# Ordering the output projection's block loads behind the kept weight parts in the SyncE queue, and moving the eight items they belong to

## The chip, the cores and the metric

The kernel runs on one core of a Trainium2 chip. The metric is the device time of one execution in microseconds (us); lower is better. Every engine of the core (TensorE = PE, VectorE = DVE, ScalarE = ACT, GpSimd = POOL, SyncE = SP) works through its own instruction stream in order and waits for the others by semaphores. Here SP issues most loads, and POOL issues most stores to device memory.

## The reference

Two decoder layers are computed on one sequence of 2048 tokens with 1024 channels. The first layer uses a gated matrix memory (mLSTM), the second a linear recurrence. What matters here is the first layer's input projection and, much later, its output projection:

```python
def mlstm_mixer(u, w_in, conv_w, conv_b, w_q, w_k, w_v, b_i, b_f, norm_w, skip, w_out):
    proj = u @ w_in
    xm, z, o_pre, i_pre, f_pre = jnp.split(proj, [...], axis=-1)
    xc = jax.nn.silu(causal_dwconv(xm, conv_w, conv_b))
    ...
    y = (hn + skip * xc) * jax.nn.silu(z)
    return y @ w_out          # (2048 x 2048) @ (2048 x 1024)
```

## The kernel before

**Numbers.** All products are float32 products made of three passes: each operand is split into a high part (a cast on ACT, L759) and a low part (a subtraction on DVE, L762), and `mm3` (L359 to L361) issues high·high, high·low and low·high.

**Products.** Each 2x2 block product uses seven block products in place of eight. This needs four sums of weight blocks, s1 to s4. Where weights serve twice, the split sums are written to device memory once and read back ("kept") later: `kept` (L96) loads 512 KB into one of eight `s` slots (L98).

**Stages.** `phase_a1` computes the input projection in two slabs of 1024 tokens. Slab 0 splits the weights and writes the sums; slab 1 reads the kept sums. In each slab, six z groups come first in two passes (an "early" pass for the first two products, then six "late" groups of five products, 60 matmuls of 512 columns each). Then the list `middle` follows, 14 items: q0, s0, q1, s2, q2, s4, q3, s6, s8, s10, s12, s14, s13, s15. A q item is a group of the o projection with 336 matmuls of 258 columns; an s item is a group of xm (even number: with a convolution on DVE) or z, with 84 matmuls of 512 columns. After `phase_a1` come the recurrence (`phase_a2`) and the second layer.

**The loads that are changed.** Slab 1 also prepares the kept sums of `w_out` for the output projection of a later stage. There are eight rounds, one per block row k. A round has two halves. `wout_blocks` (L463) loads four blocks of 256 KB into four of the eight `x` buffers (L468, on SP). `wout_sums` (L471) forms four sums on DVE (L474, in the order 21+22, 11-21, 22-11, 12-...), splits them (L759 on ACT, L762 on DVE, with four more `x` buffers), and stores eight pieces of 256 KB (L482 and L483, on POOL) to `d_ws`. The list `spread` (L623) says at which items of `middle` a round's loads are called; its sums are called at the next item, just after the weights of that item have been taken.

**What sets the order.** The order on each engine is not that of the Python calls. The tile framework's scheduler puts an instruction where it expects its inputs and its buffer to be ready. Nothing tied L468 to anything, so the scheduler was free to move it ahead of its item. The method `order(first, then)` of the kernel (L765) adds a dependency without a semaphore between two instructions of one engine: it only fixes which stands first in that engine's stream.

**Slots.** A kept load waits on SP until a matmul product has released its `s` slot, and L468 waits until its `x` buffer is free. Both stand in the one SP stream, so what is behind them waits too. On DVE the adds that empty the PSUM banks (L271 for z and s items; L560, L566 and L543 for q items) share the stream with L474.

Of the kernel before, what the change touches and what calls it, by code (L numbers as in the profile page):

```python
# [7 lines left out]
F32 = mybir.dt.float32  # L8
# [30 lines left out]
class Slab:  # L39
# [55 lines left out]

    def kept(self, keep, w=512):  # L96
        both = self.slot(w)
        self.nc.sync.dma_start(both.bitcast(F32), keep)  # L98
        return both[:, 0:w], both[:, w:2 * w]

    def weights(self, src, keep, again, part=None):
# [205 lines left out]
class Trunk:  # L307
# [74 lines left out]
    def phase_a1(self, xT, woq, wxz, wout, D):  # L382
        tc, nc = self.tc, self.nc
        with ExitStack() as ctx:
            S = Slab(self, ctx, "g0")
# [77 lines left out]
            def wout_blocks(k):  # L463

                A = {}
                for nm, kk, c in (("11", k, 0), ("21", k, 512), ("22", k + 8, 512), ("12", k + 8, 0)):
                    A[nm] = S.x()
                    nc.sync.dma_start(A[nm], wout[kk, :, c:c + 512])  # L468
                return A

            def wout_sums(k, A):  # L471
# [146 lines left out]
            for k in range(KD):  # L618
                S.scale(xs, None, pb, (k,))
                nm = ("u11", "u21")[k // 4]  # L620
                U[nm, k % 4] = S.operand(nm, k % 4, xs[k], "v")
            ew = []
            spread, sums = (0, 2, 3, 5, 7, 8, 10, 11), []  # L623
            for s in range(2):
                t = []

# [10 lines left out]
                for j, (kind, i) in enumerate(middle):  # L637
# [3 lines left out]
                    if s == 1 and j in spread:  # L641
                        sums.append((spread.index(j), wout_blocks(spread.index(j))))
# [690 lines left out]
    def phase_b2(self, rgate, rwout, D, outT):  # L1333
# [4 lines left out]
        with ExitStack() as ctx:  # L1338
# [14 lines left out]
            def fetch(kind, b, i):  # L1353

                m = 768 if kind == "g" else 512
                pool = gp if kind == "g" else wp
                keep = D["gw" if kind == "g" else "ow"][i]
                if b > 0:
                    both = pool.tile([P, 2 * m], F32R, tag="w" + kind, name="w" + kind)
                    nc.sync.dma_start(both.bitcast(F32), keep)  # L1360
                    return both[:, 0:m], both[:, m:2 * m]
                raw = pool.tile([P, m], F32, tag="wr" + kind, name="wr", bufs=2)
                nc.gpsimd.dma_start(raw, rgate[i // 2, :, i % 2 * 768:(i % 2 + 1) * 768] if kind == "g" else
                                    rwout[i % NT, :, i // NT * 512:(i // NT + 1) * 512])
                kept(1)
                both = pool.tile([P, 2 * m], F32R, tag="w" + kind, name="w" + kind)
                a = self.split_into(both[:, 0:m], both[:, m:2 * m], raw, "a", "v")
                if kind == "g" and i == 0:
                    self.order(a, self.tail[-4:])
                if kind == "r" and i == 0:  # L1370
                    self.order(self.first, a)
                stores.append((keep, both))
                if i == (7 if kind == "g" else 23):
                    kept(0)
                return both[:, 0:m], both[:, m:2 * m]
# [284 lines left out]
```

## Time and profile before

| | us |
|---|---|
| three timed runs | 3030.61 to 3032.81, median 3031.76 |
| the profiled execution, its own time | 3039.57 |
| its span, first to last instruction | 3037.8 |
| PE busy (95% of the span) | 2874.6 |
| DVE busy | 2130.9 |
| ACT busy | 1517.5 |
| POOL busy | 453.6 |

The mean granted TensorE clock of the profiled execution is 0.975 of full speed. Busy shares are means over stages that are bound by different things, so the stage of the change has to be looked at by itself: slab 1 of `phase_a1`, from about 540 to 1042 us after the span's start. The first of the 32 loads of L468 is issued at 543.8 us and the last at 675.8 us; the 32 sums of L474 run from 553.6 to 686.8 us. This is the stretch of the six late groups of slab 1.

### The profile page before, as it was taken

The page shows a single profiled execution, that of the slowest core. Times are in us where ns is not written, and L with a number is a line of the kernel's source. Part 1 is how long each engine was busy: PE and PEld are TensorE (multiplying, and loading weights), DVE is VectorE, ACT ScalarE, POOL GpSimd, SP SyncE. Part 2 cuts the span into 40 slices and gives each one's busy share as a digit, 9 for nine tenths or more (in the row PEclk, how much of TensorE's full clock was granted, in tenths as well). Part 3 has the DMA queues.
Part 4 walks back from the last instruction along what each step waited for, and adds up shares of the span by engine and source line. Part 5 has one row for each costly group of instructions (what it writes and reads, how often), then busy time and mean ns, then how long its engine had stood idle before and what let it go on. Part 6 is the DMA issues. An engine that isn't in the chain of part 4 may idle for free. (4 is left out here: it accounts for less than half of the span.)

```text
span 3037.8 us, 43242 instructions
## 1 busy us (share of the span) xinstructions
PE 2874.6 (95%) x15442; PEld 2460.0 (81%) x15442; DVE 2130.9 (70%) x3596; ACT 1517.5 (50%) x2557; POOL 453.6 (15%) x870
## 2 busy tenths in 40 slices
PE   7999999879999999999999899999999998799997
PEld 5799987659997799898999777887888886587885
DVE  7766798544447588888888755778889374766763
ACT  6344555323334466666666533435445234777760
POOL 1211132221002111111111201001221111210000
PEclk9999999989999999999999899999999999899998
DMA  6767676887667744545444567686766657778864
GB/s 225 266 217 249 234 253 235 282 315 227 218 215 232 235 147 142 166 131 169 128 146 142 193 218 281 209 272 201 255 230 217 211 185 250 260 273 298 297 203 164
DMA packets 289783, 667.70 MB, mean 220 GB/s; under 512 B 28576, under 2 KB 107168, under 8 KB 289568
## 3 DMA queue, kind: packets, MB, share of 16 engines
q1 hardware_dynamic: 219952, 422.03, 43.8%
q0 software_dynamic: 69040, 241.87, 21.1%
q8 instruction: 121, 1.98, 0.3%
q10 hardware_dynamic: 576, 1.05, 0.1%
q14 instruction: 94, 0.77, 0.1%
HBM read 427.66 MB, written 237.17 MB: 219 GB/s over the span
## 5 line engine op out<-in xcount | busy, mean ns | idle before, releaser
L759 ACT CAST s<-raw 128x512 fp32r<-128x512 f32 (+1 forms) x280 | 172.2, 621 | 267.2 <-PE pc L361 69.1
L762 DVE TENSOR_TENSOR s<-raw,s 128x512 fp32r<-128x512 f32 (+1 forms) x280 | 191.2, 688 | 53.7 <-ACT s L759 52.5
L359 PE MATMUL acc<-yh,wr 128*128 128x512 f32 x384 | 153.9, 408 | 23.3 <-DMA wr<-d_ow 8.9
L360 PE MATMUL acc<-yl,wr 128*128 128x512 f32 x384 | 155.3, 404 | 0.6 <-DVE yl L762 0.6
L361 PE MATMUL acc<-yh,wr 128*128 128x512 f32 x384 | 154.9, 403 | 0.0
L686 DVE SCALAR_TENSOR_TENSOR xc<-xm,vec,xc 128x512 f32<-128x512 f32 x192 | 139.5, 747 | 10.9 <-ACT xc L684 8.4
L759 ACT CAST u<-t 128x512 fp32r<-128x512 f32 x112 | 68.8, 619 | 154.8 <-PE pc L361 51.0
L762 DVE TENSOR_TENSOR u<-t,u 128x512 fp32r<-128x512 f32 x112 | 76.7, 689 | 85.2 <-ACT u L759 84.9
L759 ACT CAST s<-sum 128x512 fp32r<-128x512 f32 (+1 forms) x120 | 74.0, 618 | 116.0 <-PE pc L361 46.4
L359 PE MATMUL pa<-u,s 128*128 128x512 f32 x304 | 122.1, 402 | 4.6 <-ACT p L258 3.1
L360 PE MATMUL pa<-u,s 128*128 128x512 f32 x304 | 121.6, 400 | 0.0
L361 PE MATMUL pa<-u,s 128*128 128x512 f32 x304 | 121.4, 400 | 0.1
L971 DVE SCALAR_TENSOR_TENSOR C<-C,dl,kv 128x516 f32<-128x516 f32 x112 | 83.5, 746 | 48.4 <-PE kv L361 48.4
L759 ACT CAST Ch<-C 128x516 fp32r<-128x516 f32 x120 | 74.8, 623 | 84.5 <-DVE da L989 69.8
L686 DVE SCALAR_TENSOR_TENSOR xc<-xr,vec,xc 128x512 f32<-128x512 f32 x144 | 105.8, 746 | 9.2 <-ACT xc L684 8.3
L359 PEld LDWEIGHTS acc<-yh,wr 128*128 128x128 f32 x384 | 74.4, 195 | 43.3 <-issue 9.3
L359 PE MATMUL pj<-vwh,xmh 128*128 128x512 f32 x256 | 103.1, 403 | 1.9 <-ACT vwh L759 1.9
L360 PE MATMUL pj<-vwl,xmh 128*128 128x512 f32 x256 | 100.5, 393 | 0.8 <-DVE vwl L762 0.8
L361 PE MATMUL pj<-vwh,xml 128*128 128x512 f32 x256 | 100.8, 394 | 0.0
L762 DVE TENSOR_TENSOR s<-sum,s 128x512 fp32r<-128x512 f32 (+1 forms) x120 | 82.5, 688 | 25.2 <-ACT s L759 24.5
L359 PE MATMUL gate<-xch,wg 128*128 128x512 f32 x192 | 78.4, 412 | 16.9 <-ACT xch L759 11.7
L360 PEld LDWEIGHTS acc<-yl,wr 128*128 128x128 f32 x384 | 74.7, 195 | 19.2 <-DVE yl L762 1.5
(483 smaller groups left out, 10097.4 us busy)
## 6 DMA issues: line engine op xcount, KB each, us to landing
wr<-d_ow SPq DMA_DIRECT2D x72, 512.0 KB, 4.3
d_wx<-s POOLq DMA_DIRECT2D x64, 512.0 KB, 4.4
s<-d_wx SPq DMA_DIRECT2D x64, 512.0 KB, 4.7
s<-d_ws SPq DMA_DIRECT2D x64, 512.0 KB, 6.2
raw<-in_wxz_dram SPq DMA_DIRECT2D x124, 256.0 KB, 4.5
d_wr<-s POOLq DMA_DIRECT2D x48, 512.0 KB, 3.7
s<-d_wr SPq DMA_DIRECT2D x48, 512.0 KB, 4.3
raw<-in_rwin_dram SPq DMA_DIRECT2D x94, 256.0 KB, 3.9
```

What stands on the lines that cost most here:

```text
L359: mm(out, sh, mh, start=first, stop=False, skip_group_check=resumed)
L360: mm(out, sh, ml, start=False, stop=False, skip_group_check=resumed)
L361: mm(out, sl, mh, start=False, stop=last, skip_group_check=resumed)
L686: nc.vector.scalar_tensor_tensor(out, x[:, j:j + TB], self.v(wn, m * 4 + j), out, op0=ALU.mult, op1=ALU.add)
L759: a = nc.scalar.copy(hi, src)
L762: b = (nc.gpsimd if lo_eng == "p" else nc.vector).tensor_tensor(lo, src, hi.bitcast(F32), op=ALU.subtract)
L971: nc.vector.scalar_tensor_tensor(C2, C2, self.dl[:, r:r + 1], p2, op0=ALU.mult, op1=ALU.add)
```

## The change

```diff
     def kept(self, keep, w=512):
         both = self.slot(w)
-        self.nc.sync.dma_start(both.bitcast(F32), keep)
+        self.got = self.nc.sync.dma_start(both.bitcast(F32), keep)
         return both[:, 0:w], both[:, w:2 * w]
...
                 for nm, kk, c in (("11", k, 0), ("21", k, 512), ("22", k + 8, 512), ("12", k + 8, 0)):
                     A[nm] = S.x()
-                    nc.sync.dma_start(A[nm], wout[kk, :, c:c + 512])
+                    self.order((S.got,), (nc.sync.dma_start(A[nm], wout[kk, :, c:c + 512]),))
                 return A
...
-            spread, sums = (0, 2, 3, 5, 7, 8, 10, 11), []
+            spread, sums = (0, 1, 2, 4, 5, 6, 8, 10), []
```

`kept` now remembers the load it issued last (`got`). At the moment `wout_blocks` is called at item j, the weights of item j+1 have been requested as well (two items are held ready), so `got` is the last kept part (s4) of item j+1. The four loads of L468 may not stand ahead of it in SP's stream any more. The second edit moves the rounds to other items: loads at q0, s0, q1, q2, s4, q3, s8 and s12, sums at s0, q1, s2, s4, q3, s6, s10 and s14.

The scheduler's result on SP, at the start of the late groups of slab 1 (`s<-d_wx` are kept parts, L98; `raw<-in_woq_dram` are unsplit weights for q0):

```order
 L98 DMA s<-d_wx 128x1024 x3
 L424 DMA raw<-in_woq_dram 128x516
-L98 DMA s<-d_wx 128x1024 x2
-L468 DMA x<-in_wout_dram 128x512 x2
-L98 DMA s<-d_wx 128x1024
-L468 DMA x<-in_wout_dram 128x512
-L98 DMA s<-d_wx 128x1024
-L468 DMA x<-in_wout_dram 128x512
-L424 DMA raw<-in_woq_dram 128x516
```

All 32 loads of L468 stood between the kept parts of the late groups and those of q0. After the change these rows are kept parts and raw weights alone.

DVE in the first of the late groups and at the start of the second (L271 are the adds that read the PSUM banks pb, pc and pd; the split of raw weights is `s<-raw,s`):

```order
 L271 TENSOR_TENSOR u_5638<-pb,p_5276 128x512
-L474 TENSOR_TENSOR x<-x 128x512 x2
 L271 TENSOR_TENSOR p_5276<-pc,u_5638 128x512
-L474 TENSOR_TENSOR x<-x 128x512 x2
-L762 TENSOR_TENSOR x<-x 128x512
 L271 TENSOR_TENSOR z<-pd,p_5276 128x512
-L762 TENSOR_TENSOR x<-x 128x512 x3
 L271 TENSOR_TENSOR z<-pc,u_5638 128x512
 L271 TENSOR_TENSOR z<-pd,u_5638 128x512
-L474 TENSOR_TENSOR x<-x 128x512 x2
```

Sums and splits stood between the adds; now the adds stand alone there. On PE the products of the late groups stay in the same order.

SP at the change from q0 to s0, the first round's new place (`d_o<-os` are stores of the o projection, `s<-d_wq` kept parts of q1; the kept part in the second row is s4 of s0):

```order
 L530 DMA d_o<-os 128x2x256
 L98 DMA s<-d_wx 128x1024
-L530 DMA d_o<-os 128x2x256
-L83 DMA raw<-in_wxz_dram 128x512
-L424 DMA raw<-in_woq_dram 128x516 x3
+L468 DMA x<-in_wout_dram 128x512
+L83 DMA raw<-in_wxz_dram 128x512
+L468 DMA x<-in_wout_dram 128x512 x3
+L424 DMA raw<-in_woq_dram 128x516
+L530 DMA d_o<-os 128x2x256
+L424 DMA raw<-in_woq_dram 128x516 x2
 L98 DMA s<-d_wq 128x1032 x4
```

The four block loads come right behind s4 of s0, ahead of the raw weights and kept parts of q1.

DVE in s0 after the change (before it, these rows held no L474 and no `x<-x`):

```order
+L271 TENSOR_TENSOR u_6748<-pb,p_6733 128x512
+L762 TENSOR_TENSOR s<-raw,s 128x516
+L474 TENSOR_TENSOR x<-x 128x512
+L585 COPY xm<-hist 128x3
+L474 TENSOR_TENSOR x<-x 128x512 x2
+L271 TENSOR_TENSOR p_6733<-pc,u_6748 128x512
+L762 TENSOR_TENSOR s<-raw,s 128x516
+L474 TENSOR_TENSOR x<-x 128x512
+L762 TENSOR_TENSOR x<-x 128x512 x4
+L586 COPY hist<-xm 128x3
+L686 SCALAR_TENSOR_TENSOR xc<-xm,vec,xc 128x512
+L271 TENSOR_TENSOR xm<-pd,p_6733 128x512
```

Three sums now stand between the add of pb and the add of pc, and one sum, four splits and a convolution step between the add of pc and that of pd. The items s2 and s4 have the same pattern; in s6 the sums stand ahead of the add of pb, in s10 they stand among the convolution steps ahead of it, and in s14 they stand around it.

## The prediction

> **What bounds the kernel now.** I read the slices of the span first, because the busy shares alone (PE 95%) hide where PE loses time.
>
> ```profile
> PE   7999999879999999999999899999999998799997
> PEclk9999999989999999999999899999999999899998
> ```
>
> Each digit stands for a fortieth of the span, 75.9 us. PE is full nearly everywhere, so only dips are worth anything. One lies in the eighth and ninth slices (532 to 683 us), where the granted clock drops too. That is where the 32 block loads and their sums run. So I looked at this stretch item by item. Each window below runs from one item's first matmul to the next one's: the six late groups of slab 1, q0, then as measures of a clean item q1, q2 and s6. The columns are the window, its length, the busy time and count of each engine, the granted clock, the DMA share and GB/s.
>
> ```profile
> core 0: us, PE busy (x) PEld busy (x) DVE busy (x) ACT busy (x) POOL busy (x), PEclk, DMA share, GB/s
> 548.80:562.67 13.87, 13.87 (x61) 11.26 (x60) 11.70 (x19) 5.52 (x10) 5.74 (x11) 1.00 0.93 302
> 562.67:585.94 23.27, 16.18 (x62) 12.67 (x60) 8.87 (x14) 4.70 (x8) 6.62 (x13) 0.85 0.90 323
> 585.94:606.37 20.43, 15.74 (x61) 12.32 (x60) 8.08 (x13) 4.06 (x7) 5.33 (x10) 0.92 0.80 270
> 606.37:634.35 27.98, 18.44 (x61) 13.90 (x60) 14.63 (x23) 7.43 (x13) 8.69 (x17) 0.82 0.96 336
> 634.35:657.70 23.35, 15.89 (x61) 12.54 (x60) 10.27 (x16) 5.84 (x10) 7.69 (x15) 0.85 0.82 274
> 657.70:674.75 17.05, 14.19 (x61) 11.20 (x60) 9.53 (x15) 5.42 (x9) 6.12 (x12) 1.00 0.85 305
> 674.75:723.82 49.07, 42.61 (x338) 42.39 (x337) 18.01 (x40) 14.02 (x30) 4.81 (x9) 0.93 0.77 263
> 743.29:783.61 40.32, 40.32 (x337) 40.31 (x336) 18.36 (x41) 13.79 (x29) 2.15 (x4) 1.00 0.71 229
> 803.15:843.32 40.17, 40.17 (x337) 40.17 (x336) 18.35 (x41) 13.80 (x29) 2.15 (x4) 1.00 0.71 229
> 904.24:924.11 19.87, 19.87 (x88) 15.75 (x86) 15.93 (x47) 8.57 (x14) 2.15 (x4) 1.00 0.64 191
> ```
>
> A late group is 60 matmuls. The first takes 13.87 us with PE never idle; the next five take 23.27, 20.43, 27.98, 23.35 and 17.05 us for the same work, 112.08 in place of 69.35. q0 takes 49.07, where q1 and q2 take 40.25 on average. So 42.73 + 8.82 = **51.55 us** are lost here. Behind q0, PE is busy for the whole of each window.
>
> Who is waited for is in the waits, narrowed to 548 to 700 us: first PE's, then DVE's, then SP's (total, times, longest).
>
> ```profile
> PE pc L359 <- DVE p L271: 28.6, 5, 7.5
> PE oa L359 <- ACT p L554: 6.5, 1, 6.5
> PE pd L359 <- DVE z L271: 3.1, 1, 3.1
> ...
> DVE x L474 <- DMA x<-in_wout_dram: 62.2, 7, 12.9
> ...
> SPq L468 <- DMA d_ws<-x: 61.5, 19, 11.6
> ```
>
> PE waits for a DVE add; DVE has been standing at a sum whose block has not landed; the block is late because SP stood at L468 until the last round's stores to d_ws had freed an `x` buffer. One such wait, in order of time on DVE and PE:
>
> ```profile
> 573.61 1.42 DVE L474 TENSOR_TENSOR x<-x 128x512 f32<-128x512 f32 x2 [10.05 <-DMA x<-in_wout_dram]
> 574.95 0.68 DVE L271 TENSOR_TENSOR u<-pb,p 128x512 f32<-128x512 f32 x1
> ...
> 577.48 0.68 DVE L271 TENSOR_TENSOR p<-pc,u 128x512 f32<-128x512 f32 x1
> ...
> 578.30 0.77 PE L359 MATMUL pc<-t4h,s 128*128 128x512 f32 x1 [7.09 <-DVE p L271]
> ```
>
> The add of pb stood behind the sum, the add of pc behind that, and PE may not go on in pc before it is read. The adds to z in pd stand in the same stream, and ACT, whose copy q0 waits for, casts the same sums in order; I take all three rows as one cause. These idle waits make 38.2 us; the rest of the 51.55 is slower matmuls after each wait, which the clock column shows (0.82 to 0.93). After a short wait there is next to none of this: the group at 657.70 holds one wait of 2.86 us, lost 3.18, and its clock stayed at 1.00.
>
> ```profile
> 669.13 0.47 PE L359 MATMUL pc<-t4h,s 128*128 128x512 f32 x1 [2.86 <-DVE p L271]
> ```
>
> **The change, part by part.** Nothing is added or removed in amount: 32 loads, 32 sums, 32 splits and 64 stores, all moved. The handle kept by `kept` costs nothing.
>
> *What goes.* The late groups keep adds and z stores only, and SP has no L468 there. DVE's 8 to 15 us per group fall to about 4, and the first late group shows that 13.87 us is reached even with block loads under way (DMA share 0.93). I take the whole 51.55 us as gained, since nothing else there has ended a PE wait of note. What would be late next is a kept part; those had to wait in the same SP queue until now, and go ahead sooner.
>
> *What comes.* Eight rounds lie in the middle stage, where PE has no idle time: any PE wait costs in full. A round brings this much DVE work:
>
> ```profile
> L474 DVE TENSOR_TENSOR x<-x 128x512 f32<-128x512 f32 x32 | 22.1, 689 | 62.8 <-DMA x<-in_wout_dram 62.2
> L762 DVE TENSOR_TENSOR x<-x 128x512 fp32r<-128x512 f32 x32 | 20.6, 683 | 0.0
> ```
>
> Four of each make 4 x (0.689 + 0.683) = 5.49 us on DVE. The casts on ACT and the store issues on POOL fall to engines that are idle for more than half of each item.
>
> *Rounds in s0, s2, s4.* What such an item does at its second product, without a round, is shown by s2 (SP: s4 of this item, then a raw load; DVE: a split, the add of pd; PE: first matmuls that need the adds of pc and of pd).
>
> ```profile
> 783.09 0.32 SPq L98 DMA_DIRECT2D s<-d_wx  x1
> 785.24 0.42 SPq L83 DMA_DIRECT2D raw<-in_wxz_dram  x1
> ...
> 790.09 0.69 DVE L762 TENSOR_TENSOR s<-raw,s 128x516 fp32r<-128x516 f32 x1
> ...
> 797.93 0.68 DVE L271 TENSOR_TENSOR xm<-pd,p 128x512 f32<-128x512 f32 x1
> ...
> 797.55 0.39 PE L359 MATMUL pc<-t4h,s 128*128 128x512 f32 x1
> 800.35 0.40 PE L359 MATMUL pd<-u22h,s 128*128 128x512 f32 x1
> ```
>
> DVE would reach the first sum at 790.78. Three sums and the add of pc end at 793.5, against 797.55 needed. Then come a split, the fourth sum, four splits (4.1 us) and a convolution step (0.75), so the add of pd ends near 799.1, against 800.35. So 1.2 us are spare. The load that the first sum needs goes out third, near 786.3. How long do loads take? The medians from issue to landing, in the middle stage (first row) and in 540 to 700 us (second and third):
>
> ```profile
> s<-d_wx SPq DMA_DIRECT2D x40, 512.0 KB, 4.2
> ...
> x<-in_wout_dram SPq DMA_DIRECT2D x32, 256.0 KB, 7.9
> d_ws<-x POOLq DMA_DIRECT2D x64, 256.0 KB, 5.6
> ```
>
> With 4.2 us the block lands before DVE asks. With 7.9 it lands at 794.2, 3.4 us late, and PE waits 2.2. So a round costs 0 to 2.2 us; I take 0.7, nearer to the middle stage's own row, since the DMA share there is 0.64 to 0.71 and was 0.80 to 0.96 in the late groups. Three rounds: 2.1, range 0 to 6.6.
>
> *Rounds in q1 and q3.* A q item leaves DVE idle for 22 of its 40 us, and its adds sit in four banks apiece. The same bounds serve, 0 to 2.2; I take 0.5. Two rounds: 1.0, range 0 to 4.4.
>
> *Rounds in s6, s10, s14.* These have s items for neighbours. DVE is busy 15.93 of 19.87 us in s6; with 5.49 more it is 21.42, so 1.55 us too much. At best the next item's slack takes it (0); at worst it adds to a late block (1.55 + 2.2 = 3.75). I take 1.55: 4.65 for three, range 0 to 11.25.
>
> **The sum.** -51.55 + 2.1 + 1.0 + 4.65 = -43.8 us, with bounds -51.55 and -51.55 + 22.25 = -29.3. On the profiled execution's 3039.57 that is 2995.8. This execution lay 7.8 us above the median of the runs, 3031.76; I carry the difference over unchanged, so from the median the forecast is **2988**, with 2980.2 to 3002.5 from the bounds.
>
> **The rivals.**
>
> *B, the loads are slow in the middle stage as well (0.18).* The bytes moved there, with 743 to 904 us of before in the first row and 540 to 700 us in the second:
>
> ```profile
> DMA packets 16073, 35.34 MB, mean 219 GB/s; under 512 B 1618, under 2 KB 7506, under 8 KB 16059
> ...
> DMA packets 17299, 48.31 MB, mean 302 GB/s; under 512 B 2504, under 2 KB 2789, under 8 KB 17291
> ```
>
> A round moves 12 pieces of 256 KB, 3.15 MB. Five rounds in the 161 us make 35.34 + 15.7 = 51.1 MB, 317 GB/s, more than the late groups' mean. So blocks may land as late as there, and all upper bounds hold: -29.3 us, **3002**. Against it: at 229 GB/s the middle stage's DMA share is 0.71, so there is room for some 320 at a full share, and the five rounds are not all in flight at once. The Trainium skill speaks for this rival: "DMA: Bandwidth & Descriptors", section "Issuing engines are not separate DMA queues", says that transfers started by any engine share the same 16 DMA engines and interleave. By it the new place in SP's stream protects nothing from POOL's stores, and the sum would be 3002 where mine is 2988. The trace agrees so far that block loads took 7.9 us where the stores to d_ws ran.
>
> *C, SP stands at L468 again (0.08).* The closest two rounds are those that load in the middle of q1 and at the start of s2 (and likewise q3 and s6). Their places in SP's stream in before, and the first loads of two rounds in the late groups:
>
> ```profile
> 578.79 0.33 SPq L468 DMA_DIRECT2D x<-in_wout_dram  x1
> 598.64 0.33 SPq L468 DMA_DIRECT2D x<-in_wout_dram  x1
> ...
> 760.05 1.04 SPq L98 DMA_DIRECT2D s<-d_wq  x2
> ...
> 783.09 0.32 SPq L98 DMA_DIRECT2D s<-d_wx  x1
> ```
>
> The places are 23 us apart, and a turn of the `x` buffers took 19.85. With the longest group, 27.98, as the turn, two rounds are 5 us later, and the sums with them: 10 us, **2998**.
>
> *D, the late groups stay slow for another reason (0.06).* A kept part could wait for its slot there. I price it at half the gain, 26 us: **3014**, with the rounds' cost. The first late group at 13.87 us speaks against it.
>
> *E, slower than before (0.03).* The DMA engines become the bound of the middle stage. From 723.82 to 904.24 us, 180.4 us at 219 GB/s are 39.5 MB; six rounds add 18.9. At the middle stage's 229 GB/s as a ceiling, 58.4 MB take 255 us, 74.6 more than before, and 23 are left after the gain: **3055**. It decides from 252 GB/s down. The late groups moved 302, so this needs a traffic mix that is much worse.
>
> **How the numbers follow.** My case has 0.62, B 0.18, C 0.08, D 0.06, E 0.03; 0.03 is left for no change to speak of. The range 2978 to 3006 goes 2 us beyond the ceiling of the gain, about the spread of the timed runs, and covers B and C. A difference of 0.2%, 6 us, is about what a measurement of this kernel can tell from none. Faster by more: my case, B, C and D, 0.94; within it 0.03; slower 0.03.
>
> **What would show it.** Six late groups of 13.9 us and a q0 of 40.3, clock 1.00; no wait of DVE for a block before q0; in the middle stage, waits of PE for DVE of 0 to 2 us per round, most in s6, s10 and s14. It is wrong if SP's waits for d_ws go on in tens of us, if block loads take over 8 us, or if an item of the middle stage grows by more than 4 us.

## The result, and the profile after

| | before | after |
|---|---|---|
| median of the timed runs, us | 3032.28 (3030.61 to 3036.26, 4 runs) | 2995.22 (2993.59 to 2996.22, 4 runs) |
| the profiled execution, us | 3039.57 | 2996.22 |
| its span, us | 3037.8 | 2994.5 |

The ratio is 0.9875, with a 95% interval of 0.9858 to 0.9892. The medians differ by 37.1 us, the two profiled executions by 43.35.

The slices of the span of the changed kernel, PE's busy tenths and its granted clock, in fortieths of 74.9 us:

```profile
PE   7999999999999999999999899999999998699997
PEclk9999999999999999999999899999999998799998
```

The dip in the eighth and ninth slices is gone, and the clock stays up. Item by item, in the same columns as before: the first, second and last late group, q0, then q1, s2 and s6, and the whole middle stage from s0 to the start of the recurrence.

```profile
548.92:562.80 13.88, 13.88 (x61) 11.27 (x60) 6.91 (x11) 3.25 (x6) 2.17 (x4) 1.00 0.72 217
562.80:576.72 13.92, 13.92 (x61) 11.27 (x60) 4.11 (x6) 2.52 (x4) 1.63 (x3) 1.00 0.75 237
618.50:632.46 13.96, 13.96 (x62) 11.28 (x60) 4.78 (x7) 3.15 (x5) 1.63 (x3) 1.00 0.69 213
632.46:672.70 40.24, 40.24 (x338) 40.24 (x336) 13.30 (x32) 12.36 (x26) 0.54 (x1) 1.00 0.62 198
692.41:733.47 41.06, 40.57 (x337) 40.36 (x336) 23.39 (x50) 15.96 (x34) 8.22 (x16) 1.00 0.93 327
733.47:753.90 20.43, 19.80 (x86) 15.71 (x85) 13.58 (x29) 9.65 (x16) 5.37 (x10) 1.00 0.82 274
856.44:880.45 24.01, 21.84 (x89) 16.75 (x87) 19.89 (x56) 10.88 (x18) 6.48 (x12) 0.93 0.94 345
672.70:1001.29 328.59, 321.67 (x1861) 280.07 (x1859) 212.15 (x458) 143.17 (x250) 73.40 (x136) 0.99 0.85 288
```

The late groups run at 13.9 us and q0 at 40.24: 548.92 to 672.70 is 123.78 us, where the same work took 175.02 (548.80 to 723.82). That is 51.2 us gained. The middle stage took 319.60 before, in the same window (its row stands with the experiments), so 9.0 are given back. 51.2 - 9.0 = 42.2 us is nearly the whole 43.3 us by which the spans differ; the rest lies behind the start of the recurrence.

The waits of the changed kernel, from the late groups to the recurrence: PE for DVE, and DVE for a block. The second group of rows is the issues, with their size and median time to landing, from 632 to 1001 us.

```profile
PE pd L359 <- DVE xm L271: 2.8, 2, 2.2
...
DVE x L474 <- DMA x<-in_wout_dram: 12.9, 7, 3.4
```

```profile
s<-d_wx SPq DMA_DIRECT2D x40, 512.0 KB, 5.2
d_ws<-x POOLq DMA_DIRECT2D x64, 256.0 KB, 6.7
...
x<-in_wout_dram SPq DMA_DIRECT2D x32, 256.0 KB, 6.0
```

DVE still stands at seven of the eight rounds, but for 12.9 us in place of 62.2. SP no longer stands at L468 for stores to d_ws (61.5 us before): between 632 and 1001 us it waits there twice, 0.8 us together, for stores of xm. Nearly half of the 9 us are lost in s6 (24.01 us against 19.87). On DVE, in order of time:

```profile
862.89 0.69 DVE L474 TENSOR_TENSOR x<-x 128x512 f32<-128x512 f32 x1 [1.61 <-DMA x<-in_wout_dram]
...
869.04 0.67 DVE L271 TENSOR_TENSOR u<-pb,p 128x512 f32<-128x512 f32 x1
...
874.98 0.68 DVE L271 TENSOR_TENSOR xm<-pd,p 128x512 f32<-128x512 f32 x1
```

and on PE:

```profile
875.71 0.50 PE L359 MATMUL pd<-u22h,s 128*128 128x512 f32 x1 [2.17 <-DVE xm L271]
```

The add of pb comes at 869.04, 6.8 us after pb was complete (862.25), because the whole round stands ahead of it. On DVE the small operations of the gates, a split and steps of the convolution follow, so the add of pd is late too. PE waits 2.17 us for it, and the matmuls behind that run at a lower clock.

### The profile page after: what moved, and what is told of

Its sections match the earlier page's. It is cut to its first block, busy times and chain, and to the rows that moved or that the text cites. A ratio compares the mean times of both kernels' runs of the same rounds, so it can differ in the third digit from the quotient of the medians.

```text
span 2994.5 us, 43193 instructions
## 1 busy us (share of the span) xinstructions
PE 2861.5 (96%) x15442; PEld 2448.8 (82%) x15442; DVE 2127.1 (71%) x3596; ACT 1517.2 (51%) x2557; POOL 455.6 (15%) x870
## 5 line engine op out<-in xcount | busy, mean ns | idle before, releaser
L360 PE MATMUL pd<-u,s 128*128 128x512 f32 x224 | 88.5, 395 | 2.0 <-DVE u L762 2.0
```

The costliest lines, as they stand in the source:

```text
L360: mm(out, sh, ml, start=False, stop=False, skip_group_check=resumed)
```

## The experiments

Two stretches are compared throughout. The first is the six late groups with q0; the 123.78 us of the changed kernel are its clean length. The second is the middle stage, with 319.60 us in the kernel before.

| run | late groups and q0, us | over 123.8 | middle stage, us | over 319.6 | time, us |
|---|---|---|---|---|---|
| before | 175.02 | +51.2 | 319.60 | 0 | 3032.28 median |
| after | 123.78 | 0 | 328.59 | +9.0 | 2995.22 median |
| before_again | 171.66 | +47.9 | 319.59 | 0 | 3033.20 |
| spread_only | 171.15 | +47.4 | 319.87 | +0.3 | 3029.14 |
| order_only | 123.77 | 0 | 327.35 | +7.8 | 2990.52 median |
| before_no_sums | 143.42 | +19.6 | 319.85 | +0.3 | 3003.21 |
| before_no_sums_pool | 134.34 | +10.6 | 319.61 | 0 | 3000.89 |
| no_sums | 123.77 | 0 | 319.65 | 0 | 2986.03 |
| no_loads_pinned | 123.77 | 0 | 322.83 | +3.2 | 2988.52 |
| late_three | 125.32 | +1.5 | 320.16 | +0.6 | 2988.38 median |

**before_again**, the kernel before with no edit.

> The kernel before, profiled once more. The profiled execution of before lay 7.3 us above its median, that of the changed kernel 1.0 us. Theory V: the stalls of the late groups vary from execution to execution, so the late groups and q0 lose another sum here (40 to 49 us in place of 51.55) and the span is shorter by that difference, near 3031. Theory W: the stalls are fixed and the 7 us lie elsewhere in the span; then the late groups and q0 lose 51 to 52 us again.

The stretch lost 47.9 us, so the stalls do vary, by 3.3 us here. But the span is 6.6 us shorter. The other 3 us come from the part behind the input projection, which the change does not touch. From the start of the recurrence to the end it took 1994.4 us in the first profile of before and 1991.2 here; over all profiles of this study it lies between 1988 and 1995, with no relation to the edits. Both theories held in part; the span came out near the 3031 of theory V only because both parts were shorter.

**The two edits apart: order_only and spread_only.**

```diff
# order_only: the change, but
-            spread, sums = (0, 1, 2, 4, 5, 6, 8, 10), []
+            spread, sums = (0, 2, 3, 5, 7, 8, 10, 11), []
# spread_only: the kernel before, but
-            spread, sums = (0, 2, 3, 5, 7, 8, 10, 11), []
+            spread, sums = (0, 1, 2, 4, 5, 6, 8, 10), []
```

> The order of the loads as in the change, the items as before (0, 2, 3, 5, 7, 8, 10, 11). Theory A (the order alone takes the rounds out of the late groups): late groups of 13.9 us, q0 40.3, and the middle stage loses 6 to 12 us, so the time is 2993 to 3000. Rival: the items carry a good part of the gain; then the time is above 3005.

> The items of the change, without the order. Theory A: the scheduler puts the loads into the late groups as before; six late groups and q0 lose 40 to 55 us, the time is within 8 us of before. Rival: the other items alone pull some rounds into the middle stage; then the late groups lose under 30 us and the time is below 3015.

The order makes the gain by itself: 2990.52 us, ratio 0.9861 (0.9845 to 0.9878), which is 2.5 us below the range that was expected. The interval overlaps the change's own, so the new items are not shown to add or to cost anything. Without the order they do nothing: the scheduler takes all loads back into the late groups (+47.4). Where the rounds cost is different, though. With the old items the stretch up to s8 loses nothing (200.28 us against 200.29 before), though four rounds lie in it; the 7.8 us are all lost in the six s items at the end. One of the waits there, on PE:

```profile
964.66 0.79 PE L359 MATMUL pa<-u21h,s 128*128 128x512 f32 x1 [2.98 <-ACT p L281]
```

and what ACT stood at, in the waits from 955 to 966 us:

```profile
ACT x L759 <- DVE x L474: 3.7, 2, 3.3
```

and on DVE, the sum that the cast needed:

```profile
962.78 0.69 DVE L474 TENSOR_TENSOR x<-x 128x512 f32<-128x512 f32 x1 [3.41 <-DMA x<-in_wout_dram]
```

A late block reaches PE through ACT too: a cast of a sum stands ahead of the copy that PE needs.

**before_no_sums**, the kernel before without the work on the blocks.

```diff
-                comb("22", "21", "22", ALU.add)
-                comb("21", "11", "21", ALU.subtract)
-                comb("11", "22", "11", ALU.subtract)
-                comb("12", "12", "11", ALU.subtract)
...
-                    hi, lo = S.x(), A[nm]
-                    self.split_into(hi.bitcast(F32R), lo.bitcast(F32R), lo, "a", "v")
+                    hi = lo = A[nm]
```

> The kernel before, with loads and stores of all eight rounds still in the late groups, but the sums, casts and splits of these blocks left out (the raw blocks are stored in their place). Theory A (PE was held up through DVE, which stood at sums whose blocks had not landed): late groups of 13.9 us, late groups and q0 together lose under 8 us. Rival SP (kept parts came late because SP stood at block loads): the loss stays above 25 us. Rival DMA (the 48 MB of these 160 us are too much for the DMA engines): it stays above 25 us, with a DMA share near 1.

Neither came true: 19.6 us, where I expected under 8 and the rivals over 25. Without the work on the blocks about 30 of the 50 us are gone; behind it lies a second limit. Windows of the third to fifth late group, then PE's waits from 540 to 660 us:

```profile
577.95:593.52 15.57, 14.10 (x61) 11.09 (x59) 3.27 (x5) 1.88 (x3) 8.28 (x16) 1.00 1.03 404
593.52:616.64 23.12, 16.50 (x60) 12.12 (x61) 5.34 (x8) 3.69 (x6) 10.50 (x20) 0.93 1.03 406
616.64:638.03 21.39, 17.53 (x60) 13.38 (x60) 5.67 (x9) 3.93 (x7) 8.12 (x16) 0.84 1.03 405
```

```profile
PE pd L359 <- DMA s<-d_wx: 5.6, 3, 2.9
PE pb L359 <- DMA s<-d_wx: 5.2, 3, 2.8
```

PE now waits for kept parts, and the DMA engines are busy throughout at 405 GB/s. The sizes say why. A late group moves four kept parts of 512 KB, a raw block and three z stores of 256 KB, 3.15 MB; a round adds another 3.15. In 13.87 us that would be 454 GB/s, more than any of these groups reached. By this estimate a round in every late group does not fit, whatever DVE does. The 19.6 us are not simply a part of the old loss: without DVE's waits the rounds follow each other faster than in the kernel before (356 GB/s over late groups and q0, against 292), and a round holds four `x` buffers in place of eight.

**before_no_sums_pool**, the same with the loads on POOL.

```diff
-                    nc.sync.dma_start(A[nm], wout[kk, :, c:c + 512])
+                    nc.gpsimd.dma_start(A[nm], wout[kk, :, c:c + 512])
```

> The kernel before without the sums, casts and splits of the rounds (raw blocks are stored in their place), and with the block loads issued by POOL in place of SP, so that SP never stands at them. Without sums, but with the loads on SP, late groups and q0 still lost 20 us, at PE waits for kept parts. Theory SP (kept parts stood behind block loads that waited for an x buffer): under 6 us are lost here. Rival DMA (loads, stores and kept parts together are more than the DMA engines move): 12 us or more are lost, with a DMA share of 1.

10.6 us lies between the two theories. The waits of PE for kept parts are gone entirely, which is what theory SP says of them. It is not proof, because in the late groups behind the first the DMA engines also moved less (344 to 387 GB/s, where it was 404 to 414), and a kept part landed in 7.1 us in place of 10.7 (medians). The DMA share is still 0.97 to 1.02 in every group. What is left is carried by DVE's waits, from 545 to 660 us:

```profile
DVE z L271 <- DMA d_sz<-z: 29.6, 5, 11.1
```

DVE waits for the z buffers that z stores free: 40.0 us with the adds of u, where it was 24.9 in before_no_sums. The z stores share POOL's stream with the rounds' stores, which wait for their blocks there, and now with the block loads too. How the remaining loss divides between that order and the busy DMA engines stays open, and whether more `x` buffers would have helped was not tried.

**no_sums**, the changed kernel without sums, casts and splits (the same edit as in before_no_sums).

> The changed kernel with the sums, casts and splits of the eight rounds left out: the raw blocks are loaded and stored at the same places. In the changed kernel the middle stage takes 9.0 us more than it did before. Theory DVE (the price is DVE's work and its waits for blocks): the middle stage takes under 2.5 us more than before. Rival DMA (the price is the traffic of the rounds beside the kept parts): it takes 6 us more or above, with PE waits for kept parts.

The middle stage takes 319.65 us, as long as without any round. The middle stage in the kernel before:

```profile
723.82:1043.42 319.60, 317.83 (x1861) 279.05 (x1859) 178.45 (x394) 127.19 (x218) 38.96 (x72) 1.00 0.70 217
```

and in this run:

```profile
672.91:992.56 319.65, 317.88 (x1860) 279.06 (x1859) 178.80 (x394) 127.10 (x218) 73.34 (x136) 1.00 0.89 296
```

The traffic of all eight rounds is in it (296 GB/s, share 0.89) and costs PE nothing. The 9 us are made by the work on the rounds on DVE and ACT and by their waits in it.

**no_loads_pinned**, the changed kernel with sums of resident data.

```diff
-                    self.order((S.got,), (nc.sync.dma_start(A[nm], wout[kk, :, c:c + 512]),))
+                A["lo"] = S.lo
...
-                nc.vector.tensor_tensor(A[out], A[a], A[b], op=op)
+                t = nc.vector.tensor_tensor(A[out], U["u11", 0][0].bitcast(F32), U["u11", 1][0].bitcast(F32), op=op)
+                self.order((A["lo"],), (t,))
```

(`S.lo` is the last split of raw weights that was issued on DVE.)

> The changed kernel without the 32 block loads: the sums are formed of two operand tiles that are resident, and are kept behind the last split of the weights of their item by an order on DVE; casts, splits and stores stay. The 12.9 us in which DVE stood at blocks in the changed kernel are gone. Theory late block (these waits make the price): the middle stage takes under 3 us more than before. Rival work (the 5.5 us of DVE per round make it, above all where s items follow each other): it still takes 5 to 9 us more, most of it from s6 on.

3.2 us lies between the two theories. Most of it is at q3 and s6 (42.85 and 21.42 us, against 41.42 and 19.87 in before), where the gates' small operations stand beside the round: PE waits there once for 2.25 us, for a copy of the gates on DVE. So the waits for blocks, or the places that come with them, make about two thirds of the 9 us, and the work itself the rest. The sums of this run stand elsewhere on DVE, mostly at the end of q items, so the two are not separated cleanly.

**late_three**, a version of the changed kernel drawn from these runs: one round per two late groups, none in s6, s10 and s14.

```diff
                 for j, i in enumerate(first):
-                    S.group(stream(), U, out_of(i, s), p1=p1[j])
+                    W = stream()
+                    if sums:
+                        wout_sums(*sums.pop())
+                    if s == 1 and j in (0, 2, 4):
+                        sums.append((5 + j // 2, wout_blocks(5 + j // 2)))
+                    S.group(W, U, out_of(i, s), p1=p1[j])
...
-            spread, sums = (0, 1, 2, 4, 5, 6, 8, 10), []
+            spread, sums = (0, 2, 3, 5, 12), []
```

> The order of the change, but three rounds called at late groups (loads at the first, third and fifth, so one round per two groups) and five at q0, q1, s2, s4 and s13 (sums at s0, s2, q2, q3, s15; none in s6, s10 and s14). If a round in every late group was too much for the x buffers and the DMA engines, one in two fits: late groups and q0 lose under 6 us. If DVE's in-order waits alone decide, each round costs there what it did before, 6 us or more, 18 in all. With the five rounds costing 0 to 3, the time is 2983 to 2990 by the first and above 2998 by the second.

The first theory held: three rounds in the late groups cost 1.5 us together, five in the middle stage 0.6. At one round per two groups the DMA engines are asked for (2 x 3.15 + 3.15) MB in 27.7 us, 341 GB/s, and the rounds are 28 us apart. The median is 2988.38 us.

**after_5 and late_three_5**, the changed kernel and this version side by side on one chip.

> The changed kernel once more, beside the version with three rounds in the late groups, on one chip. Its input projection ended 1.3 us after 1000 us in its profile; 42 us earlier than before, against 37 us in the median of the runs. If the rest of the span varies from execution to execution by some 7 us and is not touched by the change, the ratio to before lies at 0.987 to 0.988 again, and the start of the recurrence at 1000 to 1002 us.

> The version with three rounds in the late groups and none in s6, s10 and s14, in five rounds. By its first profile the recurrence starts 6.9 us earlier than in the changed kernel (994.35 against 1001.29). If that holds in every execution, its median lies 5 to 9 us below the changed kernel's of the same job; if it was the draw of one execution, under 3 us.

The changed kernel took 2994.68 us (ratio 0.9864, 0.9848 to 0.9881, a little under the 0.987 to 0.988 expected), the version 2988.90 (0.9846, 0.9831 to 0.9860). Their runs do not overlap: 2991.93 to 2996.93 against 2985.36 to 2989.41. The recurrence starts at 1001.09 and 993.82 us, and the middle stage took 328.28 and 319.58 us. So the version beats both kernels, by 5.8 us over the change. That is within the 5 to 9 us expected if the earlier start holds in every execution.

## Why the prediction was right

The forecast was 2988 us, 43.8 below the median known then; the median came out at 2995.22, 37.1 below that of before. The way and the mechanism were right, and the gain was 6.7 us smaller than forecast.

**What goes: right in place, mis-sized for the median.** The prediction took "the whole 51.55 us as gained". In the pair of profiled executions that is what was gained (51.2). There the sum gave 2995.8 us and 2996.22 was measured, with luck: the middle stage cost 1.25 us more than forecast, and the stretch from the start of the recurrence on happened to take 1.2 us less than in before. But the 51.55 came from one execution; two other profiles with rounds in the late groups lost 47.9 and 47.4. The prediction then wrote "I carry the difference over unchanged": the profiled execution of before lay 7 us above its median, by the second profile about half of that in the stalls themselves and half behind the input projection, while the changed kernel's lay 1 us above. With 48 in place of 51.55 the same sum gives 40 us, against the 37.1 of the medians. The dearer middle stage takes 1.25 of the 3 us left; the rest is less than the timed runs of before differ among themselves.

**Why it was lost: incomplete.** "PE waits for a DVE add; DVE has been standing at a sum whose block has not landed" is what the waits showed, and taking DVE's part away gave back some 30 us. A loss of 20 appeared only then: too much traffic for a late group, and kept parts behind block loads on SP, in shares that no run separates. "What would be late next is a kept part" named it, without a price. The change removes both limits at once, so the forecast did not suffer.

**What comes: 7.75 forecast, 9.0 measured.** By items: s0, s2 and s4 cost 1.1 us (2.1 forecast); q1 and q3 cost 1.2 (1.0 forecast); q2, which has no sums of its own, lost 1.0; s6 lost 4.1 and the items behind it 1.5 (4.65 for s6, s10 and s14 together). That the sum came so near is partly luck: s0, s2, s4 and the items behind s6 cost less than forecast, and q2, which had no price, and s6 cost more. The bound for a single such round was 3.75, and growth of an item by more than 4 us was named as a sign of being wrong; s6 passed both, since the add of pb itself stood behind the round there and the gates' small operations fell into the same item. Nor was "after a short wait there is next to none of this" safe: in s6 PE was idle for 2.17 us but lost 4.14, and the granted clock of the item was 0.93. In the second profile of the changed kernel (after_5) PE waited 2.20 us at the same matmul and 1.09 us at an earlier one, and s6 took 23.71 us with the clock at 1.00.

**The rivals.** B put all loads at 7.9 us; they took 6.0, between that and 4.2, so DVE did wait for blocks, though the sum had them land before DVE asks. The traffic alone cost nothing (no_sums). The rule of the Trainium skill that speaks for B ("DMA: Bandwidth & Descriptors", section "Issuing engines are not separate DMA queues": the DMAs of all issuing engines run on the same 16 DMA engines) agrees with the landing times, which rose for kept parts too (4.2 to 5.2 us). It does not decide here, because the kept parts that landed later still landed in time for PE. C did not occur: SP has no wait at L468 for d_ws any more. D did not occur. E was far off: it took 229 GB/s as a ceiling, and before_no_sums shows 405. Even the "some 320 at a full share" that was held against B was too low.

## What to carry to other kernels

A load that depends on nothing is placed by the scheduler wherever its queue looks free, and takes its consumers with it into whatever stretch that is; fixing its order behind the loads it belongs with is enough to move the whole chain, and here that one edit was the gain. Before moving such a chain, divide the bytes of a group by its clean length and compare with the highest rate that a run has shown: a stretch that cannot carry one round per group may well carry one per two. When one wait explains a loss, take that wait away by itself before believing it explains all of it: a second limit can lie hidden behind the first.

## What the runs showed of the hardware

The DMA engines moved 404 to 406 GB/s at a share of 1.03 over three late groups of before_no_sums, though at 229 GB/s their share was already 0.71: the share does not grow in proportion to the rate, and an extrapolation from it put the ceiling 20% too low. Packets of one size took less time at the higher rate: those of 4 KB in SP's queue 207 ns on average in q1 of the kernel before, and 162 ns in those three groups. And 79 GB/s more in the middle stage (296 against 217) cost PE nothing, with a share of 0.89.

The length of a short wait does not tell whether PE's clock drops. After 2.86 us of waiting in the kernel before, the granted clock stayed at 1.00 over the group; after 2.17 us in s6 of the changed kernel it was 0.93 over the item, and the matmuls behind the wait made up 2 us of the loss. After 2.20 us at the same matmul in after_5 it stayed at 1.00.
